# A hybrid decoder layer with a dense product-key expert stage: one-hot tiles stored token by token, lookups four places side by side, gate matrices in groups of 8 chunks

## The chip, the cores and the metric

The kernel runs on one core of one Trainium2 chip. A core has a matrix engine (TensorE, PE in the profile; PEld is its weight load), a vector engine (VectorE, DVE), a scalar engine (ScalarE, ACT), GpSimd (POOL) and a sync engine (SP) that only issues transfers. The metric is the device time of one execution in microseconds (us); lower is better. Before the change it was 1528.64 us, the median of 3 runs (1527.38 to 1529.46).

## What is computed (the reference)

One layer on 512 tokens of width 1024: a mixer (a short gated convolution and a gated linear recurrence side by side), then an expert stage whose "experts" are single neurons. The change lies in the expert stage alone:

```python
q = (xt @ wq).reshape(t, PEER_HEADS, 2, HALF_Q)                    # 8 heads, two halves each
scores = jnp.einsum('thpd,hpnd->thpn', q, keys)                    # 128 keys for each half
s_top, i_top = lax.top_k(scores, PEER_TOPK)                        # 16 best of each half
cand = s_top[:, :, 0, :, None] + s_top[:, :, 1, None, :]           # 16 x 16 pairs
c_score, c_idx = lax.top_k(cand, PEER_TOPK)                        # 16 best pairs
i1 = take_along_axis(i_top[:, :, 0], c_idx // 16); i2 = take_along_axis(i_top[:, :, 1], c_idx % 16)
expert = i1 * 128 + i2;  gates = softmax(c_score)
a = gelu(x . u_tab[expert]);  y = sum_k gates * a * v_tab[expert]  # 16384 experts, 8 x 16 per token
```

## The kernel before

There are four blocks of 128 tokens. Block 0 gathers the rows of its experts from u and v by indirect transfers (`gu`, `gv`, issued by GpSimd, computed on VectorE). Blocks 1 to 3 (TD = 384 tokens) are computed densely: all 16384 experts stand in 128 chunks of 128, and a matrix of gates G[token, expert], mostly zeros, weights them. Every fp32 product runs as three fp32r matmuls of split operands (`mm3`, L113; `split`, L96, makes the halves with one ScalarE and one VectorE instruction of 1024 columns).

- `uchunk(c)` (L439): loads 512 KB of u, splits it, 24 matmuls of 384 columns, a gelu on ScalarE. The result of the first 84 chunks (`SPILL`) goes to memory (`Ad`).
- `pick` and `lookup` (L543, L588): the top 16 pairs, then the two key numbers of each by a one-hot product: a [128, 16] tile `oh` (128 places, 16 candidates each) is compared, multiplied by the candidates' numbers `tif` and added up in halves.
- `gate_t(tb)` (L619) transposes key numbers and gates so that a partition is one of the 8 x 16 choices and a column a token, in fp16, with the gate in a high and a low part (tile `gt`).
- `gate_m(tb, b)` (L632), 24 calls: for 16 tokens it builds one-hot tiles in fp16 with four VectorE instructions (L643 to L646): `A` marks the first key, `B1` and `B2` the second key times the gate's high and low part. For each token two matmuls of 128x128 (L654, L655; `A` is the stationary operand, `B2` and `B1` are streamed) give its 128x128 gates; four tokens share a PSUM tile, which ScalarE copies to `stg` (L657). Every second call writes 2 MB to memory (`Gd`).
- The last stage (L757 on): chunks 84 to 127, then 0 to 83. `gload` brings gates of 4 chunks (768 KB) into a tile `Gt` (3 buffers); `vchunk` (L736) loads 512 KB of v, multiplies the gelu result by the gates (L742), splits it (L745, L747), and 18 matmuls of 512 columns add to six PSUM tiles. For the first 41 chunks of this stage a `uchunk` runs beside.

The program is written in a dependency framework: a scheduler reorders the instructions of each engine at build time, tiles take a pool's buffers and give them back after their last reader, and every engine then runs its list strictly in order. The list `work` (L702) interleaves u chunks with gate calls, `UOFF` (L43) says how many u chunks are kept back for after them, and 48 of the 256 gathers lie there too. In `gate_m` a token t of group q sits at `[:, q, :, t]` of a tile [128, 4, 128, 4], so one token's 128 values lie 4 elements (8 bytes) apart.

Of the kernel before, what the change touches and what calls it, by code (L numbers as in the profile page):

```python
# [21 lines left out]
P = 128  # L22
T = 512
# [16 lines left out]
TAIL = 4  # L40
EARLY = 48
PACE = (2.65, 1.1)
UOFF = 5  # L43
MRING = 12
STARTS = (16, 24, 29, 33, 36, 38, 40)
STEPS = (16, 8, 5, 4, 3, 2, 2)
# [7 lines left out]
def body(ctx, tc, a):  # L54
    nc = tc.nc
    V, S, G, PE = nc.vector, nc.scalar, nc.gpsimd, nc.tensor
# [8 lines left out]
    dr = sb("dr", space=DRAM)  # L65
# [53 lines left out]
    hT = (hp.tile([P, ND, T], F32R, tag="hi", name="hThi"), hp.tile([P, ND, T], F32R, tag="lo", name="hTlo"))  # L119
    x1d = dr.tile([NB, P, D], F32, name="x1d")  # L120
    h2d = dr.tile([P, D], F32, name="h2d")
    Gd = dr.tile([NK // 4, P, TD // CH, 4, CH], F32, name="Gd")
    Ad = dr.tile([SPILL, P, TD], F32, name="Ad")

    mp = sb("mp", 2)
# [262 lines left out]
    c = conv_c(0)  # L388
    for tb in range(NB):
        hgrn_pre(tb)  # L390
    for tb in range(NB):
# [8 lines left out]
        if tb < NB - 1:  # L400
            c = conv_c(tb + 1)
# [186 lines left out]
    def lookup(tb, j, picked):  # L588
        pa, pb, gs = picked
        idx = []  # L590
        for p_, pos in ((0, pa), (1, pb)):
            pos = pos[:, j * H * K:(j + 1) * H * K]
            ti = s2.tile([P, H, K], F16, tag="tif", name="tif")
            V.tensor_copy(ti, topi[tb][:, :, p_, :])
            oh = sp.tile([P, H * K, K], F16, tag="oh", name="oh")
            V.tensor_tensor(oh, pos.unsqueeze(2).to_broadcast([P, H * K, K]),
                            iota16[:, None, :].to_broadcast([P, H * K, K]), OP.is_equal)
            oh4 = oh.rearrange("p (h k) j -> p h k j", h=H)
            V.tensor_mul(oh4, oh4, ti.unsqueeze(2).to_broadcast([P, H, K, K]))
            V.tensor_add(oh[:, :, 0:8], oh[:, :, 0:8], oh[:, :, 8:16])  # L600
            V.tensor_add(oh[:, :, 0:4], oh[:, :, 0:4], oh[:, :, 4:8])
            V.tensor_add(oh[:, :, 0:2], oh[:, :, 0:2], oh[:, :, 2:4])
            ix = sp.tile([P, H * K], F32, tag="ix%d" % p_, name="ix")
            V.tensor_add(ix, oh[:, :, 0], oh[:, :, 1])
            idx.append(ix)
        return idx[0], idx[1], gs[j]

# [5 lines left out]
    gt = {}  # L613
# [5 lines left out]
    def gate_t(tb):  # L619
        i1, i2, g = lookup(tb, tb - 1, picked[0])  # L620
        o = ps()
        for j, t in enumerate((i1, i2, g)):
            PE.transpose(o[:, j * P:(j + 1) * P], t, ident)
        r = s2.tile([P, 4, P], F16, tag="gt", name="gt")
        S.activation(r[:, 0:2, :].rearrange("p a b -> p (a b)"), o[:, 0:2 * P], AF.Copy)
        S.activation(r[:, 2, :], o[:, 2 * P:3 * P], AF.Copy, scale=GSC)
        V.scalar_tensor_tensor(r[:, 3, :], o[:, 2 * P:3 * P], GSC, r[:, 2, :], op0=OP.mult, op1=OP.subtract)
        gt[tb] = r

    stg = {}  # L630

    def gate_m(tb, b):  # L632

        r = gt[tb]

        def view(j):
            return r[:, j, b * 16:(b + 1) * 16].rearrange("p (q t) -> p q t", t=4).unsqueeze(2).to_broadcast(
                [P, 4, NK, 4])
        io = iota4[:, None, :, :].to_broadcast([P, 4, NK, 4])
        A = s2.tile([P, 4, NK, 4], F16, tag="A", name="A")  # L640
        B1 = s2.tile([P, 4, NK, 4], F16, tag="B1", name="B1")
        B2 = s2.tile([P, 4, NK, 4], F16, tag="B2", name="B2")
# [218 lines left out]
```

## Time and profile before

| | |
|---|---|
| median of 3 runs | 1528.64 us |
| the profiled execution, its own time | 1528.5 us |
| its span, first to last instruction | 1526.7 us, mean granted clock 0.994 |
| busy: PE, PEld, DVE | 1502.8 (98%), 1338.8 (88%), 1213.2 (79%) us |
| busy: ACT, POOL | 638.8 (42%), 365.1 (24%) us |
| moved | 394.75 MB, mean 259 GB/s |

Busy time is the union of an engine's records. Each matmul's record is longer than its share of the engine, because matmuls overlap; what one costs in a stream is the distance from start to start. An idle stretch of an engine counts only where that engine ends last.

### The profile page before, as it was taken

The numbers are of one execution on the slowest core, as the hardware profiler recorded it, in microseconds if no ns is written. First come the engines' busy times: TensorE is split into PE (matmuls) and PEld (weight loads), VectorE is DVE, ScalarE is ACT, GpSimd is POOL, SyncE is SP. The second block draws the span as 40 slices with busy tenths as digits, with TensorE's granted clock in tenths as the row PEclk, the third lists the DMA queues.
The fourth block names the chain that finished last, engine by engine and source line by source line (L and its number), as shares of the span: only waits on it lengthen the run. The fifth ranks groups of instructions, "written<-read, shape, count | busy, mean of one in ns | idle before, by whom it ended". The sixth has DMA issues, their size and how long they took to land.

```text
span 1526.7 us, 21785 instructions
## 1 busy us (share of the span) xinstructions
PE 1502.8 (98%) x7929; PEld 1338.8 (88%) x7929; DVE 1213.2 (79%) x2312; ACT 638.8 (42%) x900; POOL 365.1 (24%) x300
## 2 busy tenths in 40 slices
PE   7999999999999999999999999999999999999997
PEld 6887777889999999999999999999998888888886
DVE  5847876899989988786646877888788888888888
ACT  5833324333543364655653333333333333333333
POOL 0000000000043311222004444444443332433330
PEclk9999999999999999999999999999999999999999
DMA  6221234523469788698759998988989999999993
GB/s 232 84 97 56 69 114 164 201 84 101 169 217 380 250 268 260 219 310 258 238 168 404 381 336 312 330 326 321 357 323 346 364 364 354 363 351 356 344 331 143
DMA packets 164652, 394.75 MB, mean 259 GB/s; under 512 B 13248, under 2 KB 84416, under 8 KB 164416
## 3 DMA queue, kind: packets, MB, share of 16 engines
q1 hardware_dynamic: 47520, 170.94, 30.8%
q0 software_dynamic: 41472, 159.40, 28.8%
q10 hardware_dynamic: 75552, 63.01, 13.0%
q8 instruction: 62, 1.02, 0.3%
q14 instruction: 46, 0.38, 0.1%
HBM read 346.90 MB, written 46.40 MB: 258 GB/s over the span
## 4 chain that ended last, share of the span: by engine, by line
PE 91%; DVE 5%; DMA 2%; ACT 1%; issue 1%; POOL 0%; DVEq 0%; ACTq 0%; SPq 0%; POOLq 0%
PE y L115 11%; PE y L116 11%; PE y L114 11%; PE pa L114 10%; PE pa L116 10%; PE pa L115 10%; PE pm L114 6%; PE pm L115 6%; PE pm L116 6%; PE pm L654 3%; PE pm L655 3%; DVE wlo L100 1%; PE pm L537 1%; DMA wraw<-in_u_dram,e_i 1%; PE pm L301 1%; DMA wraw<-in_v_l_dram 1%
## 5 line engine op out<-in xcount | busy, mean ns | idle before, releaser
L98 ACT ACTIVATE whi<-wraw 128x1024 fp32r<-128x1024 f32 x308 | 325.7, 1057 | 507.6 <-PE pa L115 199.0
L100 DVE TENSOR_TENSOR wlo<-wraw,whi 128x1024 fp32r<-128x1024 f32 x308 | 376.6, 1223 | 155.0 <-ACT whi L98 139.5
L114 PE MATMUL pa<-h2Thi,whi 128*128 128x384 f32 x1024 | 346.5, 338 | 4.1 <-ACT gl L446 4.1
L116 PE MATMUL pa<-h2Thi,wlo 128*128 128x384 f32 x1024 | 346.1, 338 | 0.0
L115 PE MATMUL pa<-h2Tlo,whi 128*128 128x384 f32 x1024 | 345.8, 338 | 0.0
L116 PE MATMUL y<-whi,wl 128*128 128x512 f32 x768 | 299.4, 390 | 0.0
L115 PE MATMUL y<-wlo,wh 128*128 128x512 f32 x768 | 299.3, 390 | 0.0
L114 PE MATMUL y<-whi,wh 128*128 128x512 f32 x768 | 297.9, 389 | 0.0
L673 POOL DMA_INDIRECT wraw<-in_u_dram,e_i x128 | 167.5, 1309 | 482.4 <-DMA Ad<-gl 178.4
L673 POOL DMA_INDIRECT wraw<-in_v_dram,e_i x128 | 175.4, 1370 | 303.5 <-DVE wlo L100 134.4
L114 PEld LDWEIGHTS pa<-h2Thi,whi 128*128 128x128 f32 x1024 | 193.9, 189 | 7.0 <-ACT gl L446 5.1
L115 PEld LDWEIGHTS pa<-h2Tlo,whi 128*128 128x128 f32 x1024 | 194.0, 189 | 1.6
L116 PEld LDWEIGHTS pa<-h2Thi,wlo 128*128 128x128 f32 x1024 | 193.8, 189 | 0.0
L687 DVE SCALAR_TENSOR_TENSOR y<-wraw,w,y 128x1024 f32<-128x1024 f32 x128 | 163.7, 1279 | 14.7 <-DMA wraw<-in_v_dram,e_i 14.6
L116 PEld LDWEIGHTS y<-whi,wl 128*128 128x128 f32 x768 | 144.2, 188 | 30.0
L745 ACT ACTIVATE wh<-w 128x384 fp32r<-128x384 f32 x128 | 67.0, 524 | 245.8 <-PE y L115 134.9
L114 PEld LDWEIGHTS y<-whi,wh 128*128 128x128 f32 x768 | 144.2, 188 | 29.1
L115 PEld LDWEIGHTS y<-wlo,wh 128*128 128x128 f32 x768 | 144.2, 188 | 29.0
L679 DVE SCALAR_TENSOR_TENSOR wraw<-wraw,h2n 128x1024 f32<-128x1024 f32 x128 | 155.8, 1219 | 15.2 <-DMA wraw<-in_u_dram,e_i 15.2
L747 DVE TENSOR_TENSOR wl<-w,wh 128x384 fp32r<-128x384 f32 x128 | 71.2, 557 | 41.7 <-ACT wh L745 38.2
L657 ACT ACTIVATE stg<-pm 128x512 f32<-128x512 f32 x96 | 94.2, 1162 | 21.5 <-PE pm L655 20.8
L654 PE MATMUL pm<-B,A 128*128 128x128 f16 x384 | 91.3, 297 | 0.0
(242 smaller groups left out, 1807.0 us busy)
## 6 DMA issues: line engine op xcount, KB each, us to landing
wraw<-in_u_l_dram SPq DMA_DIRECT2D x128, 512.0 KB
wraw<-in_v_l_dram SPq DMA_DIRECT2D x128, 512.0 KB
Gd<-stg ACTq DMA_DIRECT2D x12, 2048.0 KB
Gt<-Gd POOLq DMA_DIRECT2D x32, 768.0 KB
Ad<-gl ACTq DMA_DIRECT2D x84, 192.0 KB
glr<-Ad ACTq DMA_DIRECT2D x84, 192.0 KB
wraw<-in_w_in_dram SPq DMA_DIRECT2D x24, 512.0 KB
wraw<-in_wq_dram SPq DMA_DIRECT2D x16, 512.0 KB
```

The costliest lines, as they stand in the source:

```text
L98: S.activation(hi, src, AF.Copy)
L100: V.tensor_sub(lo, src, hi.bitcast(F32))
L114: PE.matmul(out, l[0], r[0], start=first, stop=False)
L115: PE.matmul(out, l[0], r[1], start=False, stop=False)
L116: PE.matmul(out, l[1], r[0], start=False, stop=last)
L654: PE.matmul(o3[:, t, :], A[:, q, :, t], B2[:, q, :, t], start=True, stop=False)
L657: S.activation(st[:, t0:t0 + 4, :], o3, AF.Copy, scale=1.0 / GSC)
L673: G.indirect_dma_start(out=t, out_offset=None, in_=a[tab], in_offset=bass.IndirectOffsetOnAxis(ap=e_i32[:, j:j + 1], axis=0))
L679: V.scalar_tensor_tensor(r, r, 1.0, h2n, op0=OP.mult, op1=OP.mult, accum_out=act0[:, j:j + 1])
L687: V.scalar_tensor_tensor(y0, r, w0[:, j:j + 1], y0, op0=OP.mult, op1=OP.add)
L745: S.activation(wh, w, AF.Copy)
L747: V.tensor_sub(wl, w, wh.bitcast(F32))
```

## The change

One-hot tiles are stored [128, 16 tokens, 64, 2]: the 128 values of a token lie side by side. The number that VectorE compares with is held twice in `gt` (the three instructions of `gate_t` that fill it write both copies), so that the innermost run is two equal fp16 values read again 64 times. In `lookup` the 16 candidates of four places lie side by side ([32, 16, 4]), and the sum ends one halving earlier. `Gd` and `Gt` hold 8 chunks in a group (`GC`), `Gt` has 2 buffers of 1536 KB in place of 3 of 768 KB, and `UOFF` goes from 5 to 8. `keys` moves into a buffer of `stg`.

```diff
-UOFF = 5
+GC = 8
+UOFF = 8
-    Gd = dr.tile([NK // 4, P, TD // CH, 4, CH], F32, name="Gd")
+    Gd = dr.tile([NK // GC, P, TD // CH, GC, CH], F32, name="Gd")
-    keys = sp.tile([P, NHP, NK], F32, name="keys")
+    keys = s2.tile([P, NHP, NK], F32, tag="stg", name="keys")
...
-            ti = s2.tile([P, H, K], F16, tag="tif", name="tif")
-            V.tensor_copy(ti, topi[tb][:, :, p_, :])
-            oh = sp.tile([P, H * K, K], F16, tag="oh", name="oh")
-            V.tensor_tensor(oh, pos.unsqueeze(2).to_broadcast([P, H * K, K]),
-                            iota16[:, None, :].to_broadcast([P, H * K, K]), OP.is_equal)
+            ti = s2.tile([P, H, K, 4], F16, tag="tif", name="tif")
+            V.tensor_copy(ti, topi[tb][:, :, p_, :].unsqueeze(3).to_broadcast([P, H, K, 4]))
+            oh = sp.tile([P, H * K // 4, K * 4], F16, tag="oh", name="oh")
+            V.tensor_tensor(oh.rearrange("p q (j r) -> p q j r", r=4),
+                            pos.rearrange("p (q r) -> p q r", r=4).unsqueeze(2).to_broadcast([P, H * K // 4, K, 4]),
+                            iota16.rearrange("p (j r) -> p j r", r=4).unsqueeze(1).to_broadcast(
+                                [P, H * K // 4, K, 4]), OP.is_equal)
...
-            V.tensor_add(oh[:, :, 0:8], oh[:, :, 0:8], oh[:, :, 8:16])
-            V.tensor_add(oh[:, :, 0:4], oh[:, :, 0:4], oh[:, :, 4:8])
-            V.tensor_add(oh[:, :, 0:2], oh[:, :, 0:2], oh[:, :, 2:4])
+            for n in (32, 16, 8):
+                V.tensor_add(oh[:, :, 0:n], oh[:, :, 0:n], oh[:, :, n:2 * n])
-            V.tensor_add(ix, oh[:, :, 0], oh[:, :, 1])
+            V.tensor_add(ix.rearrange("p (q r) -> p q r", r=4), oh[:, :, 0:4], oh[:, :, 4:8])
...
-        r = s2.tile([P, 4, P], F16, tag="gt", name="gt")
+        r = s2.tile([P, 4, P, 2], F16, tag="gt", name="gt")
+        o2 = o.unsqueeze(2).to_broadcast([P, T, 2])
...
-            return r[:, j, b * 16:(b + 1) * 16].rearrange("p (q t) -> p q t", t=4).unsqueeze(2).to_broadcast(
-                [P, 4, NK, 4])
+            return r[:, j, b * 16:(b + 1) * 16, :].unsqueeze(2).to_broadcast([P, 16, NK // 2, 2])
+        io = iota.rearrange("p (i r) -> p i r", r=2).unsqueeze(1).to_broadcast([P, 16, NK // 2, 2])
+        A, B1, B2 = (s2.tile([P, 16, NK // 2, 2], F16, tag=t, name=t) for t in ("A", "B1", "B2"))
...
-                PE.matmul(o3[:, t, :], A[:, q, :, t], B2[:, q, :, t], start=True, stop=False)
-                PE.matmul(o3[:, t, :], A[:, q, :, t], B1[:, q, :, t], start=False, stop=True)
+                one = [m[:, 4 * q + t].rearrange("p i r -> p (i r)") for m in (A, B2, B1)]
+                PE.matmul(o3[:, t, :], one[0], one[1], start=True, stop=False)
+                PE.matmul(o3[:, t, :], one[0], one[2], start=False, stop=True)
...
-        Gt[g] = vp.tile([P, TD // CH, 4, CH], F32, tag="G", name="Gt", bufs=3)
+        Gt[g] = vp.tile([P, TD // CH, GC, CH], F32, tag="G", name="Gt", bufs=2)
...
-    gload(order[0] // 4)
-    gload(order[0] // 4 + 1)
+    gs_ = []
+    for c in order:
+        if c // GC not in gs_:
+            gs_.append(c // GC)
+    gload(gs_[0])
+    used = []
     for n, c in enumerate(order):
-        if n % 4 == 0 and n // 4 + 2 < NK // 4:
-            gload(order[n + 8] // 4)
+        if c // GC not in used:
+            used.append(c // GC)
+            if len(used) < len(gs_):
+                gload(gs_[len(used)])
```

The built order on TensorE around the gate calls keeps its pattern: runs of 58 gate matmuls, and 6 a little ahead, for two calls. Elsewhere it moves at three places.

The first is GpSimd's list at the start of the last stage, where it loads the gates (`Gt`) ahead of the gathers of expert rows (`wraw`). Before:

```order
L734 DMA Gt_7904<-Gd_84 128x1536
L734 DMA Gt_7906<-Gd_84 128x1536
L734 DMA Gt_7908<-Gd_84 128x1536
L673 DMA wraw_7973<-in_u_dram,e_i32_2158 128x1024
L673 DMA wraw_7976<-in_v_dram,e_i32_2158 128x1024
```

And now:

```order
L736 DMA Gt_7904<-Gd_84 128x3072
L736 DMA Gt_7906<-Gd_84 128x3072
L675 DMA wraw_7971<-in_u_dram,e_i32_2158 128x1024
L675 DMA wraw_7974<-in_v_dram,e_i32_2158 128x1024
L675 DMA wraw_8040<-in_u_dram,e_i32_2158 128x1024
```

Three loads of 4 chunks become two of 8; 14 more follow, in place of 29.

The second is VectorE's list late in the last stage: `w` is the product with the gates (`glr` is the gelu result read back), `wl` and `wlo` are low halves of splits, `y0` is block 0's work. Before:

```order
L742 TENSOR_TENSOR w_13499<-glr_13491,Gt_13094 128x384
L747 TENSOR_TENSOR wl_13465<-w_13461,wh_13463 128x384
L100 TENSOR_TENSOR wlo_13459<-wraw_13455,whi_13457 128x1024
L679 SCALAR_TENSOR_TENSOR wraw_13523,act0_2160<-wraw_13523,h2n_2162 128x1024
L742 TENSOR_TENSOR w_13538<-glr_13530,Gt_13239 128x384
L747 TENSOR_TENSOR wl_13503<-w_13499,wh_13501 128x384
```

And now:

```order
L749 TENSOR_TENSOR wl_13473<-w_13469,wh_13471 128x384
L101 TENSOR_TENSOR wlo_13467<-wraw_13463,whi_13465 128x1024
L689 SCALAR_TENSOR_TENSOR y0_2163<-wraw_13600,w0_2161,y0_2163 128x1024
L689 SCALAR_TENSOR_TENSOR y0_2163<-wraw_13635,w0_2161,y0_2163 128x1024
L101 TENSOR_TENSOR wlo_13504<-wraw_13500,whi_13502 128x1024
L101 TENSOR_TENSOR wlo_13539<-wraw_13535,whi_13537 128x1024
L744 TENSOR_TENSOR w_13506<-glr_13498,Gt_13211 128x384
L744 TENSOR_TENSOR w_13541<-glr_13533,Gt_13211 128x384
L744 TENSOR_TENSOR w_13576<-glr_13568,Gt_13211 128x384
L744 TENSOR_TENSOR w_13611<-glr_13603,Gt_13211 128x384
L101 TENSOR_TENSOR wlo_13574<-wraw_13570,whi_13572 128x1024
```

Before, one product stood among each chunk's other work. Now four stand in a row, and the first of a group comes after the work on the group before it.

The third is the end of VectorE's list of these products. Now:

```order
L689 SCALAR_TENSOR_TENSOR y0_2163<-wraw_13846,w0_2161,y0_2163 128x1024
L689 SCALAR_TENSOR_TENSOR y0_2163<-wraw_13849,w0_2161,y0_2163 128x1024
L101 TENSOR_TENSOR wlo_13804<-wraw_13800,whi_13802 128x1024
L689 SCALAR_TENSOR_TENSOR y0_2163<-wraw_13852,w0_2161,y0_2163 128x1024
L744 TENSOR_TENSOR w_13786<-glr_13778,Gt_7904 128x384
L744 TENSOR_TENSOR w_13806<-glr_13798,Gt_7904 128x384
L744 TENSOR_TENSOR w_13823<-glr_13815,Gt_7904 128x384
L744 TENSOR_TENSOR w_13840<-glr_13832,Gt_7904 128x384
```

The last four chunks (80 to 83) belong to the group that was loaded first (`Gt_7904`, chunks 80 to 87). That tile keeps one of the two buffers through the whole stage, so the 14 groups after the second pass one after another through the other buffer: GpSimd's load of a group waits for VectorE's eighth product of the one before (`Gt_8190` and those after it have such a wait; the first two have none of it).

## Rows read from the trace of the kernel before

**Rows 1.** The page, busy time by engine (share of the span, instructions).

```profile
PE 1502.8 (98%) x7929; PEld 1338.8 (88%) x7929; DVE 1213.2 (79%) x2312; ACT 638.8 (42%) x900; POOL 365.1 (24%) x300
```

**Rows 2.** Windows: length, busy us of PE, PEld, DVE, ACT, POOL, clock, DMA share.

```profile
370.00:430.00 60.00, 60.00 (x348) 60.00 (x347) 60.00 (x345) 27.41 (x35) 0.00 (x0) 1.00 0.49 164
515.00:600.00 85.00, 85.00 (x550) 82.57 (x549) 73.49 (x77) 44.65 (x54) 20.51 (x11) 1.00 0.77 251
515.00:787.00 272.00, 272.00 (x1808) 263.58 (x1807) 206.06 (x202) 155.28 (x187) 50.75 (x23) 1.00 0.77 245
820.00:1162.00 342.00, 342.00 (x1735) 311.79 (x1734) 279.54 (x350) 126.22 (x172) 151.12 (x123) 1.00 0.92 339
1162.00:1503.00 341.00, 341.00 (x1506) 282.47 (x1505) 287.91 (x380) 124.43 (x171) 116.80 (x107) 1.00 0.95 349
```

**Rows 3.** Chain that ended last, 515 to 790 us, shares by line.

```profile
by line: PE pa L114 22.3%; PE pa L116 22.3%; PE pa L115 22.2%; PE pm L654 16.6%; PE pm L655 16.5%; PE pm L623 0.2%
```

**Rows 4.** Timeline of PE in a gate run: start, length (us).

```profile
661.01 0.30 PE L654 MATMUL pm<-B,A 128*128 128x128 f16 x1
...
661.96 0.30 PE L655 MATMUL pm<-B,A 128*128 128x128 f16 x1
```

**Rows 5.** Timeline of PE, 384 columns; 25 steps from first to last.

```profile
650.06 0.33 PE L114 MATMUL pa<-h2Thi,whi 128*128 128x384 f32 x1
...
654.39 0.33 PE L115 MATMUL pa<-h2Tlo,whi 128*128 128x384 f32 x1
```

**Rows 6.** Timeline of PE, 512 columns; 8 steps from first to last.

```profile
1300.03 0.39 PE L116 MATMUL y<-whi,wl 128*128 128x512 f32 x1
...
1301.84 0.39 PE L115 MATMUL y<-wlo,wh 128*128 128x512 f32 x1
```

**Rows 7.** Weight loads of single lines, ns: least/median/most.

```profile
L655 PEld LDWEIGHTS <-A x384: 112/117/135, 535.8 to 785.8; 128*128 128x128 f16 x192
L285 PEld LDWEIGHTS pm<-Q,E x32: 190/192/192, 105.9 to 110.7; 128*128 128x128 f32 x32
L320 PEld LDWEIGHTS po<-F,Q x64: 106/108/109, 119.6 to 202.8; 128*32 128x32 f32 x64
```

**Rows 8.** Timeline of PE, eight fp32 matmuls merged: start, length.

```profile
106.01 1.06 PE L285 MATMUL pm<-Q,E 128*128 128x128 f32 x8
```

**Rows 9.** Groups by line: count, busy us, mean ns, idle before.

```profile
L657 ACT ACTIVATE stg<-pm 128x512 f32<-128x512 f32 x96 | 94.2, 1162 | 21.5 <-PE pm L655 20.8 <-ACT gl L446 0.4 <-issue 0.3
L643 DVE TENSOR_TENSOR A<-iota,gt 128x2048 f16<-128x2048 f16 x24 | 29.3, 1223 | 20.1 <-PE pm L655 18.3 <-ACT gt L625 1.8
L596 DVE TENSOR_TENSOR oh<-pb,iota 128x2048 f16<-128x2048 f16 x4 | 9.2, 2294 | 0.1
L602 DVE TENSOR_TENSOR oh<-oh 128x256 f16<-128x256 f16 x8 | 3.6, 446 | 0.0
L601 DVE TENSOR_TENSOR oh<-oh 128x512 f16<-128x512 f16 x8 | 3.5, 442 | 0.0
L604 DVE TENSOR_TENSOR ix<-oh 128x128 f32<-128x128 f16 x8 | 3.4, 429 | 5.9 <-PE pm L623 5.9
```

**Rows 10.** Windows behind a wait of PE: columns as in Rows 2.

```profile
450.00:455.00 5.00, 1.91 (x12) 1.59 (x10) 5.00 (x13) 3.03 (x4) 4.09 (x4) 0.92 0.65 206
455.00:460.00 5.00, 5.00 (x16) 5.00 (x17) 5.00 (x14) 1.44 (x2) 3.80 (x4) 0.50 0.88 275
```

**Rows 11.** The gate products of the last 84 chunks: first and last start.

```profile
L742 DVE TENSOR_TENSOR w<-glr,Gt x84: 546/553/561, 1162.2 to 1502.7; 128x384 f32<-128x384 f32 x84
```

**Rows 12.** Chain of waits, 425 to 470 us: a 512 KB gather landing.

```profile
430.40 4.50 DMA wraw<-in_u_dram,e_i
```

**Rows 13.** Chain of waits, 787 to 830 us: a 512 KB load landing.

```profile
807.84 9.30 DMA wraw<-in_v_l_dram
```

More of the change, by code (lines that the diff above doesn't have):

```diff
@@ L505, in ps @@
         return psS.tile([P, T], F32, tag="m", name="pm")
-    keys = sp.tile([P, NHP, NK], F32, name="keys")
+    keys = s2.tile([P, NHP, NK], F32, tag="stg", name="keys")
     S.dma_start(out=keys, in_=a["keys"])
-    iota4 = sp.tile([P, NK, 4], F16, name="iota4")
-    S.dma_start(out=iota4, in_=a["iota4"])
-    iota16 = sp.tile([P, K + 240], F16, name="iota16")[:, 0:K]
+    iota = sp.tile([P, NK + 128], F16, name="iota")[:, 0:NK]
+    S.dma_start(out=iota, in_=a["iota"])
+    iota16 = sp.tile([P, 4 * K + 192], F16, name="iota16")[:, 0:4 * K]
     S.dma_start(out=iota16, in_=a["iota16"])
@@ L592, in lookup @@
             pos = pos[:, j * H * K:(j + 1) * H * K]
-            ti = s2.tile([P, H, K], F16, tag="tif", name="tif")
-            V.tensor_copy(ti, topi[tb][:, :, p_, :])
-            oh = sp.tile([P, H * K, K], F16, tag="oh", name="oh")
-            V.tensor_tensor(oh, pos.unsqueeze(2).to_broadcast([P, H * K, K]),
-                            iota16[:, None, :].to_broadcast([P, H * K, K]), OP.is_equal)
-            oh4 = oh.rearrange("p (h k) j -> p h k j", h=H)
-            V.tensor_mul(oh4, oh4, ti.unsqueeze(2).to_broadcast([P, H, K, K]))
-            V.tensor_add(oh[:, :, 0:8], oh[:, :, 0:8], oh[:, :, 8:16])
-            V.tensor_add(oh[:, :, 0:4], oh[:, :, 0:4], oh[:, :, 4:8])
-            V.tensor_add(oh[:, :, 0:2], oh[:, :, 0:2], oh[:, :, 2:4])
+            ti = s2.tile([P, H, K, 4], F16, tag="tif", name="tif")
[5 more added lines that the diff above has]
+                                [P, H * K // 4, K, 4]), OP.is_equal)
+            oh4 = oh.rearrange("p (h q) x -> p h q x", h=H)
+            V.tensor_mul(oh4, oh4, ti.rearrange("p h j r -> p h (j r)").unsqueeze(2).to_broadcast(
+                [P, H, K // 4, K * 4]))
+            for n in (32, 16, 8):
+                V.tensor_add(oh[:, :, 0:n], oh[:, :, 0:n], oh[:, :, n:2 * n])
             ix = sp.tile([P, H * K], F32, tag="ix%d" % p_, name="ix")
-            V.tensor_add(ix, oh[:, :, 0], oh[:, :, 1])
+            V.tensor_add(ix.rearrange("p (q r) -> p q r", r=4), oh[:, :, 0:4], oh[:, :, 4:8])
             idx.append(ix)
@@ L623, in gate_t @@
             PE.transpose(o[:, j * P:(j + 1) * P], t, ident)
-        r = s2.tile([P, 4, P], F16, tag="gt", name="gt")
-        S.activation(r[:, 0:2, :].rearrange("p a b -> p (a b)"), o[:, 0:2 * P], AF.Copy)
-        S.activation(r[:, 2, :], o[:, 2 * P:3 * P], AF.Copy, scale=GSC)
-        V.scalar_tensor_tensor(r[:, 3, :], o[:, 2 * P:3 * P], GSC, r[:, 2, :], op0=OP.mult, op1=OP.subtract)
+        r = s2.tile([P, 4, P, 2], F16, tag="gt", name="gt")
+        o2 = o.unsqueeze(2).to_broadcast([P, T, 2])
+        S.activation(r[:, 0:2].rearrange("p a b r -> p (a b) r"), o2[:, 0:2 * P], AF.Copy)
+        S.activation(r[:, 2], o2[:, 2 * P:3 * P], AF.Copy, scale=GSC)
+        V.scalar_tensor_tensor(r[:, 3], o2[:, 2 * P:3 * P], GSC, r[:, 2], op0=OP.mult, op1=OP.subtract)
         gt[tb] = r
@@ L636, in view @@
         def view(j):
-            return r[:, j, b * 16:(b + 1) * 16].rearrange("p (q t) -> p q t", t=4).unsqueeze(2).to_broadcast(
-                [P, 4, NK, 4])
[L639 to L642, printed above, removed]
+            return r[:, j, b * 16:(b + 1) * 16, :].unsqueeze(2).to_broadcast([P, 16, NK // 2, 2])
+        io = iota.rearrange("p (i r) -> p i r", r=2).unsqueeze(1).to_broadcast([P, 16, NK // 2, 2])
+        A, B1, B2 = (s2.tile([P, 16, NK // 2, 2], F16, tag=t, name=t) for t in ("A", "B1", "B2"))
         V.tensor_tensor(A, io, view(0), OP.is_equal)
@@ L647, in gate_m @@
         if b % 2 == 0:
-            stg[0] = s2.tile([P, NK // 4, 4, CH], F32, tag="stg", name="stg")
+            stg[0] = s2.tile([P, NK // GC, GC, CH], F32, tag="stg", name="stg")
         st = stg[0].rearrange("p g c t -> p t (g c)")
@@ L742, in vchunk @@
         V.tensor_mul(w.rearrange("p (b t) -> p b t", t=CH), gl.rearrange("p (b t) -> p b t", t=CH),
-                     Gt[c // 4][:, :, c % 4, :])
+                     Gt[c // GC][:, :, c % GC, :])
         wh = vp.tile([P, TD], F32R, tag="wh", name="wh", bufs=4)
@@ L849 @@
         scanm=c(np.broadcast_to((np.arange(T) % CH != 0).astype(np.float32), (P, T))),
-        iota4=c(np.broadcast_to(pos[None, :, None], (P, P, 4)).astype(np.float16)),
-        iota16=c(np.broadcast_to(np.arange(K)[None, :], (P, K)).astype(np.float16)),
+        iota=c(np.broadcast_to(pos[None, :], (P, P)).astype(np.float16)),
+        iota16=c(np.broadcast_to(np.repeat(np.arange(K), 4)[None, :], (P, 4 * K)).astype(np.float16)),
     )
```

## The prediction

> **What bounds the kernel now.** I read the page first: TensorE is busy for 98% of the span, VectorE for 79%, ScalarE for 42% [rows 1]. An engine at 98% over the whole span leaves one question to the windows: is it so in the stage that is changed? It is. Between 515 and 787 us, where all gate calls lie, TensorE is busy for 272 of 272 us, VectorE for 206 and ScalarE for 155; in the last stage (820 to 1503 us) TensorE is again never idle, VectorE is at 82 to 84% and the DMA engines at 92 to 95% [rows 2]. The chain of waits confirms that busy means bound: from 515 to 790 us it runs through TensorE alone, and 33.1% of it, 91.0 us, are the two gate matmul lines L654 and L655 [rows 3]. So a microsecond taken from those lines is a microsecond of the kernel, until VectorE, ScalarE or a transfer becomes late instead; and a microsecond of VectorE in this stage is worth nothing yet.
>
> **The change part by part.**
>
> *Gate matmuls (768, L654 and L655).* 91.0 us over 768 is 118.5 ns each. The timeline agrees: eight steps from 661.01 to 661.96 us are 119 ns each [rows 4]. What would they cost with the 128 values side by side? No fp16 matmul with adjacent values is in the trace, so I take the nearest streams, the fp32r ones, whose values are adjacent: 384 columns take 4.33 us over 25 steps, 173.2 ns [rows 5]; 512 columns take 1.81 over 8, 226.3 ns [rows 6]. That is 0.415 ns for a column and 14 ns beside; for 128 columns the line gives 67 ns. A gate matmul costs 51 ns more than this, about another 128 x 0.415: it streams at half the rate. Its weight load could forbid 67 ns: its record is 117 ns [rows 7], suspiciously near the 118.5. But a record of a load holds latency that overlaps: the fp32 load of 128 columns has 192 ns, yet eight such matmuls follow each other in 1.06 us, some 112 ns apart [rows 7, 8]. Of fp32 loads 32 columns take 108 ns and 128 take 192, so some 80 ns are fixed [rows 7]; that leaves 37 of the 117 ns for occupying the array, under 67. I take 67 ns: 768 x 51.5 = 39.6 us saved. The bounds are 118.5 (nothing saved) and 0.415 x 128 = 53 ns (50 us).
>
> [...]
>
> *Gate tiles on VectorE (96 instructions, L643 to L646).* Same element counts, 2048 each. Now the broadcast number is read as a run of four fp16 values again and again, at 1.22 us [rows 9]; then it is a run of two. An instruction whose broadcast operand has no such run (L596, one value read 16 times) takes 2.29 us for the same 2048 [rows 9]. These are the bounds: no change, or 96 x 1.07 = 103 us more. I take no change, since two adjacent values still fill the pair that the faster rate handles; it is the nearer row.
>
> *Lookups (8 one-hot products).* L596 gets a run of four and should fall from 2.29 to the 1.22 us of L643: 8.6 us of VectorE. The last two additions lose their short runs (446 and 429 ns [rows 9]); at best they become a third cheaper, 2 us together. The cast that fills `tif` grows from 128 to 512 elements: at most the 0.44 us of L601 for 512, 3.5 us in all [rows 9]. Net some 5 to 10 us of VectorE, worth nothing on the path: even where VectorE has no free time (370 to 430 us) TensorE stays full [rows 2].
>
> *gate_t and the copies to `stg`.* Six instructions write twice as many values; the 96 copies of 1162 ns [rows 9] keep their pattern. Nothing.
>
> *What is late next in the gate stage.* 272 - 40 = 232 us of TensorE stand against VectorE's 206 less 3 lookup pairs, some 200 us, and ScalarE's 155. On average TensorE still ends last. It is tight at the start: from 515 to 600 us VectorE has 73 of 85 us [rows 2], and TensorE would give up 10 to 13. I add 3 us for waits there (0 to 10). Against it works that VectorE itself waited 18.3 us for TensorE to free `A` [rows 9]; that shrinks. UOFF moves three u chunks from the stage to behind it, but the built order has only one chunk more between the last gate matmul and the first v matmul: nothing.
>
> *Gate loads in groups of 8.* Bytes stay, loads become 16 of 1536 KB. But `Gt_7904` holds a buffer to the end, so from the third group on a load starts only when VectorE's eighth product is done. How much cover has it? In the last 84 chunks a chunk takes (1502.7 - 1162.2)/83 = 4.10 us [rows 11]. The products come in fours; behind the eighth, VectorE still owes splits and low halves for four chunks and TensorE has these four to run, 16 us, plus the rest of the four before. I count 20 us from the load's issue until TensorE runs dry. The landing: 512 KB take 4.5 us in a quiet stretch [rows 12] and 9.3 in the most crowded one [rows 13]; three times that is 13.5 to 28 us. I take 14 to 18: covered, with 2 us in all for stragglers. In the first 41 chunks each takes twice as long, so the cover doubles there.
>
> *Sum.* The profiled execution took 1528.5 us (span 1526.7 and 1.8 around it), 0.1 below the median of the runs, so I sum against it: 1528.5 - 39.6 + 3 + 2 = 1494 us.
>
> **The rivals.**
>
> *One buffer for the gates is too few.* Ten loads fall in the last 84 chunks. If a load lands at the upper bound, 28 us, each leaves 8 us of TensorE idle: 80 us, 1574. For it: the DMA engines are 95% busy there [rows 2] and gathers queue on the same GpSimd list. Against: the same traffic feeds TensorE without any gap now, and while VectorE waits, the other loads fill their buffers and stop. [...] I price this case at 2.5 us a load: 1494 + 25 - 2 = 1517. It turns slower from 3.6 us a load on.
>
> *VectorE loses its fast rate on runs of two (the slower case).* Then 200 + 103 = 303 us of VectorE stand in the gate stage and TensorE no longer bounds it: 303 in place of 272, 1528.5 + 31 = 1560. For it: L602, whose runs are pairs, takes 446 ns for 256 elements, while L601 takes 442 for 512 [rows 9], so pairs went at half rate there. Against: L604, single values 32 bytes apart, needs 429 ns for 128 [rows 9], so distance alone slows a read, and the gate tiles have none: the pair is read again in place, the rest is contiguous. Slower begins where VectorE passes 272 us, at (272 - 200)/96 = 0.75 us more per instruction.
>
> *The stride is not why the stream is slow.* If each gate matmul waits for its own 117 ns load, or fp16 streams so in any layout, nothing is saved: 1528.5 + 0 to 3, no change. For it: 117 beside 118.5. Against: the fp32 loads above. [...]
>
> **How the numbers follow.** The sum holds: 69%, 1483 (53 ns a matmul) to 1503 (waits of 10 us in the gate stage and 4 in the last one). One buffer too few: 13%, 1503 to 1574, mostly under 1520 (10 faster, 1 same, 2 slower). Slow pairs: 9%, slower. No gain: 9% (7 same; 2 faster, where only a part of the rate comes back). The range for 8 in 10 is 1482 to 1520; outside lie slow pairs, no gain and the worst of the single buffer. About 0.2% (3 us) can be told from no change. Faster: 69 + 10 + 2 = 81%. Same: 1 + 7 = 8%. Slower: 9 + 2 = 11%.
>
> **What would show it.** Right: L654 and L655 start some 67 ns apart and their records fall from 0.30 us [rows 4] to about 0.23; L643 to L646 stay at 1.22 us and L596 falls to it; TensorE's gate stage takes 230 to 240 us, and it stays at 100% after 820 us. Wrong: gate matmuls still 118 ns apart (no gain); L643 to L646 near 2.3 us with TensorE waiting for `B` (slow pairs); in the last stage, VectorE waiting for a `Gt` transfer every eighth chunk and TensorE idle behind it (one buffer).

## The result and the profile after

The changed kernel takes 1499.96 us (median of 6 runs, 1497.07 to 1507.19), the one before 1528.61 (6 runs on the same chip). The medians lie 28.6 us apart. The ratio, which is taken of the means, is 0.9826, with a 95% interval from 0.9801 to 0.9851: 1.7% faster. The forecast was 1494, its range 1482 to 1520. The profiled execution took 1500.03 us, its span 1498.1.

Line numbers have moved: the gate matmuls are L656 and L657 now, the gate tiles L644 to L647, the copies to `stg` L659, the gelu L447, its store to `Ad` L449, `mm3` L115 to L117, the products of the last stage L744.

First the gate matmuls. The timeline of PE in a gate run (start, length in us) answers to [rows 4]:

```profile
705.34 0.22 PE L656 MATMUL pm<-B,A 128*128 128x128 f16 x1
705.40 0.22 PE L657 MATMUL pm<-B,A 128*128 128x128 f16 x1
705.46 0.22 PE L656 MATMUL pm<-B,A 128*128 128x128 f16 x1
```

They start some 56 ns apart (the median over the run; the times here are rounded to 10 ns) where they started 119 apart. The groups by line, 300 to 850 us (count, busy us, mean ns of one, idle time before), answer to [rows 7, 9]:

```profile
L657 PEld LDWEIGHTS <-A 128*128 128x128 f16 x384 | 34.9, 98 | 2.0 <-issue 1.9
L644 DVE TENSOR_TENSOR A<-iota,gt 128x2048 f16<-128x2048 f16 x24 | 29.3, 1221 | 6.3 <-ACT gt L629 4.3 <-PE pm L657 2.0
L597 DVE TENSOR_TENSOR oh<-pb,iota 128x2048 f16<-128x2048 f16 x4 | 4.9, 1216 | 0.0
L659 ACT ACTIVATE stg<-pm 128x512 f32<-128x512 f32 x96 | 92.3, 1156 | 17.7 <-PE pm L657 17.7
```

VectorE's gate tiles with runs of two cost 1.22 us, what runs of four did [rows 9], the lookups' compare fell from 2.29 to 1.22 us, and the copies to `stg` are as before (1156 ns, 1162 [rows 9]).

The windows (length, busy us of PE, PEld, DVE, ACT, POOL, clock, DMA share) answer to [rows 2]:

```profile
515.00:600.00 85.00, 82.01 (x626) 78.79 (x625) 74.44 (x79) 48.13 (x59) 27.79 (x10) 1.00 0.84 283
515.00:760.00 245.00, 234.36 (x1826) 224.67 (x1825) 198.35 (x198) 154.90 (x188) 53.37 (x22) 0.99 0.79 272
794.00:1136.00 342.00, 342.00 (x1730) 311.22 (x1729) 277.20 (x345) 123.40 (x169) 149.57 (x119) 1.00 0.91 334
1136.00:1478.00 342.00, 341.79 (x1509) 282.65 (x1508) 287.71 (x382) 124.97 (x174) 115.17 (x96) 1.00 0.93 347
```

TensorE was full in the matching windows before [rows 2]. Now it is full, to 0.2 us, in the last stage alone, and lacks 10.6 us between 515 and 760. The waits of PE from 515 to 850 us (total us, times, longest) say for what:

```profile
PE pa L115 <- ACT gl L447: 8.2, 7, 3.2
PE pm L656 <- DVE B L646: 1.8, 1, 1.8
PE pm L657 <- DVE B L647: 0.3, 1, 0.3
```

`gl` is the gelu that empties the PSUM buffer of a u chunk; the kernel before has one such wait in this stretch and no other:

```profile
PE pa L114 <- ACT gl L446: 1.0, 1, 1.0
```

The chain of waits ran through TensorE alone before [rows 3]. Now, from 525 to 752 us, ScalarE's copies are its largest line, with 24.6%, and TensorE's matmuls together hold 57%:

```profile
by line: ACT stg L659 24.6%; PE pa L115 17.0%; PE pa L116 16.1%; PE pa L117 16.0%; issue 4.9%; DMA Gd<-stg 4.8%; PE pm L656 4.3%; PE pm L657 3.4%; ACTq L449 2.7%; ACT gl L447 2.2%; ACT whi L99 1.1%; ACTq L662 0.7%; DVE A L644 0.5%; DVE wlo 
```

Why a gelu of 0.48 us is late shows in the timeline of ScalarE around the longest wait (ACTq is its queue issuing a DMA):

```profile
619.82 7.68 ACT L659 ACTIVATE stg<-pm 128x512 f32<-128x512 f32 x8 [1.77 <-PE pm L657]
627.53 0.38 ACTq L662 DMA_DIRECT2D Gd<-stg  x1
628.01 0.49 ACT L447 ACTIVATE gl<-pa 128x384 f32<-128x384 f32 x1 [0.51 <-ACT stg L659]
628.53 6.08 ACTq L449 DMA_DIRECT2D Ad<-gl  x1
634.71 1.06 ACT L99 ACTIVATE whi<-wraw 128x1024 fp32r<-128x1024 f32 x1 [5.26 <-issue]
635.67 0.47 ACT L447 ACTIVATE gl<-pa 128x384 f32<-128x384 f32 x1
636.18 0.35 ACTq L449 DMA_DIRECT2D Ad<-gl  x1
```

Two things can hold it. Copies stand in rows of up to eight ahead of it, and behind the store of the gates (L662) the issue of the next small store (L449) takes 6.08 us instead of the 0.35 of the one after it, with everything on ScalarE behind it. TensorE then starts at 636.20 after 3.19 us without work, and pays again:

```profile
635.00:640.00 5.00, 3.80 (x12) 3.70 (x12) 5.00 (x6) 2.58 (x4) 0.00 (x0) 0.54 1.06 393
```

The granted clock of these 5 us is 0.54; behind the wait of [rows 10] it was 0.50. The blocked issue is no child of the change. Before, it is there behind every one of the 12 stores, 2.9 to 5.2 us each, 51 us together. One of them, in the timeline of ScalarE of the kernel before:

```profile
544.66 0.38 ACTq L660 DMA_DIRECT2D Gd<-stg  x1
...
546.61 5.10 ACTq L448 DMA_DIRECT2D Ad<-gl  x1
```

It cost nothing there: from 545 to 553 us TensorE ran matmuls of u chunks without a gap. That it is the slow gate matmuls which left ScalarE this time is shown by e7 below. After the change an issue in this stage exceeds 0.8 us 8 times, 18 us together. Each store writes rows of 1 KB in place of 512 bytes; on the queue that carries them, q10, packets fell from 75552 to 50976:

```profile
q10 hardware_dynamic: 50976, 62.93, 11.9%
```

**Where the time went.** I add up TensorE's steps (start of a matmul to start of the next) from 300 us on, in three heaps: steps from a gate matmul, steps over 0.4 us (waits, and what the start behind them costs), and all others. The same for every run below. It is one profiled execution of each, up to 6 us from the median of its runs:

```
profiled run                          gate   long  other    span (us)
before                                87.3    5.2  1125.6  1526.7
after                                 42.4   21.1  1124.8  1498.1
e1  token tiles alone                 42.1   42.1  1127.6  1522.3
e2  after, groups of 4                42.4   32.5  1124.6  1507.8
e3  after, store on SyncE             43.0   20.6  1124.2  1497.6
e4  after, copies in runs of 4        42.7   21.6  1124.6  1498.6
e5  after, UOFF 5                     45.3   36.7  1123.6  1515.4
e6  after, old lookups                42.6   26.0  1122.9  1501.5
e7  after, moving operand strided     85.6    5.7  1124.4  1525.6
e8  after, stationary one strided     43.3   25.1  1124.0  1502.4
e9  after, old one-hot tiles          87.5    7.0  1121.1  1525.4
e10 e3 and e4 together                42.8   11.5  1124.6  1488.7
e11 e10, fewer early gathers          43.5   28.9  1125.3  1507.9
e12 e1, with the edits of e10         42.7   19.8  1126.8  1499.8
```

From before to after the gate matmuls give 44.9 us, and 15.9 come back as long steps: 29.0 net, against 28.6 in the span.

### The profile page after: what moved, and what is told of

It is laid out like the page before. It is cut to its first block, busy times and chain, and to the rows that moved or that the text cites. A ratio compares the mean times of both kernels' runs of the same rounds, so it can differ in the third digit from the quotient of the medians.

```text
span 1498.1 us, 21741 instructions
## 1 busy us (share of the span) xinstructions
PE 1462.3 (98%) x7929; PEld 1297.3 (87%) x7929; DVE 1201.3 (80%) x2312; ACT 637.0 (43%) x900; POOL 365.8 (24%) x284
## 3 DMA queue, kind: packets, MB, share of 16 engines
q10 hardware_dynamic: 50976, 62.93, 11.9%
## 4 chain that ended last, share of the span: by engine, by line
PE 76%; DVE 6%; ACT 5%; issue 5%; DMA 5%; POOL 2%; ACTq 1%; POOLq 0%; DVEq 0%
PE y L116 10%; PE y L115 10%; PE y L117 10%; PE pa L115 8%; PE pa L116 7%; PE pa L117 7%; PE pm L115 7%; PE pm L116 6%; PE pm L117 6%; ACT stg L659 4%; DMA wraw<-in_v_dram,e_i 2%; POOL wraw L675 2%; DVE wlo L101 2%; DMA wraw<-in_u_dram,e_i 1%; PE pm L538 1%
## 5 line engine op out<-in xcount | busy, mean ns | idle before, releaser
L115 PE MATMUL pa<-h2Thi,whi 128*128 128x384 f32 x1024 | 348.0, 340 | 12.7 <-ACT gl L447 12.4
L117 PE MATMUL pa<-h2Thi,wlo 128*128 128x384 f32 x1024 | 346.6, 338 | 0.0
L675 POOL DMA_INDIRECT wraw<-in_u_dram,e_i x128 | 183.3, 1432 | 490.2 <-DVE ci L523 178.6
L115 PE MATMUL y<-whi,wh 128*128 128x512 f32 x768 | 298.9, 389 | 0.2 <-ACT wh L747 0.2
L117 PE MATMUL y<-whi,wl 128*128 128x512 f32 x768 | 296.8, 390 | 0.0
L675 POOL DMA_INDIRECT wraw<-in_v_dram,e_i x128 | 169.4, 1323 | 263.2 <-DVE wlo L101 122.0
L115 PEld LDWEIGHTS pa<-h2Thi,whi 128*128 128x128 f32 x1024 | 194.3, 190 | 17.8 <-ACT gl L447 15.9
L117 PEld LDWEIGHTS pa<-h2Thi,wlo 128*128 128x128 f32 x1024 | 194.1, 190 | 0.0
L117 PEld LDWEIGHTS y<-whi,wl 128*128 128x128 f32 x768 | 144.1, 188 | 30.2
L115 PEld LDWEIGHTS y<-whi,wh 128*128 128x128 f32 x768 | 144.2, 188 | 29.7 <-ACT wh L747 0.6
L659 ACT ACTIVATE stg<-pm 128x512 f32<-128x512 f32 x96 | 92.3, 1156 | 17.7 <-PE pm L657 17.7
L115 PE MATMUL pm<-hThi,whi 128*128 128x512 f32 x192 | 77.7, 406 | 8.4 <-ACT whi L99 8.4
```

The costliest lines, as they stand in the source:

```text
L115: PE.matmul(out, l[0], r[0], start=first, stop=False)
L117: PE.matmul(out, l[1], r[0], start=False, stop=last)
L675: G.indirect_dma_start(out=t, out_offset=None, in_=a[tab], in_offset=bass.IndirectOffsetOnAxis(ap=e_i32[:, j:j + 1], axis=0))
```

## The experiments

Theory: reading the moving operand in place brings 45 us; waits of TensorE in the gate stage, mostly for what ScalarE's queue holds up, take a share of it back, and the other three edits decide how large that share is. Rivals: the token tiles are all that matters; the single spare gate buffer took the rest; VectorE did. Each run has a ratio to the kernel before on its own chip, and where it is set against the changed kernel, that is done by these ratios. The lists of the engines are built anew for every variant. By line and tile TensorE's list is the changed kernel's in e4, e7 and e8, and in e2 up to 1140 us; in the others it differs in the gate stage.

**e1, the token tiles alone** (kernel before with the new `gate_t` and `gate_m`; lookups, groups of 4 and UOFF 5 stay):

```diff
-                PE.matmul(o3[:, t, :], A[:, q, :, t], B2[:, q, :, t], start=True, stop=False)
+                one = [m[:, 4 * q + t].rearrange("p i r -> p (i r)") for m in (A, B2, B1)]
+                PE.matmul(o3[:, t, :], one[0], one[1], start=True, stop=False)
```

> Kernel before with the token-by-token one-hot tiles alone (old lookups, groups of 4 chunks, UOFF 5). Theory: the tiles bring the gate matmuls to the full rate (records 0.22 us, about 40 us less of TensorE), but the store of the gate matrices keeps its 512-byte rows, behind which ScalarE's issue of the spilled gelu was held up 3 to 5 us after each of the 12 stores in the kernel before (only up to 6 us in 5 places after). TensorE, no longer slowed by the stride, now waits for the gelu behind them: 1503 to 1512 us, 18 to 25 less than before, longer than the changed kernel. Rival A, only the tiles matter and the groups of 8 are worth nothing: 1498 to 1502. Rival B, the layout is not the source of the gain: about 1528.

Measured: 1526.53 us, ratio 0.9996 (0.9980 to 1.0013): no change, as rival B had it. But the table denies B's reason. The gate matmuls are at full rate (42.1 us), and 36.9 us stand against them in long steps. Waits of PE, 515 to 850 us, then the longest on ScalarE's side and the clock behind it:

```profile
PE pa L114 <- ACT gl L446: 21.0, 17, 7.5
PE pm L653 <- ACT stg L656: 4.3, 3, 2.4
```

```profile
640.25 10.37 ACTq L448 DMA_DIRECT2D Ad<-gl  x1
```

```profile
645.00:650.00 5.00, 0.00 (x0) 0.00 (x0) 4.46 (x4) 0.00 (x0) 0.00 (x0) 0.87 1.12 373
650.00:655.00 5.00, 2.79 (x9) 2.79 (x10) 3.19 (x3) 2.87 (x4) 1.68 (x1) 0.50 0.89 329
```

All 12 issues behind a store are blocked again, 3.7 to 10.4 us each, 56 us in all. The theory had the place right and the size too small. (3.8 us of the waits lie at the very end, 1474 to 1499 us; they are in e12 too.)

**e2, groups of 4 again** (`GC = 4`, three `Gt` buffers, loads two groups ahead).

> Changed kernel with the gate matrices in groups of 4 chunks again (three buffers, loads two groups ahead). Theory: twice as many store rows, ScalarE's issues behind the stores are held up 3 to 5 us at all 12, TensorE's waits in the gate stage grow from about 10 to 15 or 20 us: 1504 to 1512. Rival A: regrouping is worth nothing either way, 1498 to 1502. Rival C, the single spare Gt buffer costs time in the changed kernel: then this kernel is faster, under 1497.

Measured: 1509.89 us, ratio 0.9896 (0.9875 to 0.9917), some 11 us slower than the changed kernel. So rival C falls: with three buffers it is not faster. TensorE's list in the gate stage is the same here, so no new order on TensorE explains the loss. The waits for the gelu are 19.1 us in place of 8.2, and again 12 issues are blocked, 51 us together:

```profile
PE pa L115 <- ACT gl L447: 19.1, 16, 5.4
PE pm L656 <- ACT stg L659: 2.4, 2, 2.1
```

**e5, UOFF 5, and e6, the old lookups,** each put back alone in the changed kernel.

> Changed kernel with UOFF 5 in place of 8 (three more u chunks lie among the gate calls). The token tiles alone measured 1526.5 us and the changed kernel with groups of 4 1509.9; between these two lie only UOFF and the lookups, 16 us. Theory now: both kernels lose the same 40 us of gate matmuls and differ in TensorE's waits for the gelu and the slow clock behind them. Theory U, UOFF is what tells: each u chunk moved out of the stage takes its gelu, its split and its issue off ScalarE and VectorE there, so with 5 the waits grow from 10.6 to some 18 to 20 us: 1506 to 1512. Theory L, the lookups tell: no change from the changed kernel, 1498 to 1502.

> Changed kernel with the old lookups (single values, 2.29 us for the compare). Theory U (UOFF explains the 16 us): VectorE does 8 to 10 us more, TensorE's waits grow by 0 to 3 us: 1499 to 1503. Theory L (the lookups, whose 10 us lie just ahead of a third of the gate calls each, are what VectorE lacks): 1508 to 1514.

Measured: e5 1511.50 us, ratio 0.9890 (0.9861 to 0.9920), about 10 us slower than the changed kernel; e6 1505.36, ratio 0.9877 (0.9852 to 0.9903), about 8 us slower, with an interval that begins 0.0001 above the end of the changed kernel's. Neither theory U nor L alone holds: putting back either costs time. But TensorE's list differs from the changed kernel's at some 20 places in either, so each price is that of the edit together with its new order. In e5 it is mostly VectorE that is late: 15.6 us of TensorE's 20.9 us of waits are for it, 5.3 for ScalarE (waits of PE, 515 to 850 us; then VectorE's own, 515 to 760 us):

```profile
PE pm L656 <- DVE B L646: 11.7, 8, 6.1
```

```profile
DVE wraw L681 <- DMA wraw<-in_u_dram,e_i: 24.8, 7, 7.8
DVE y L689 <- DMA wraw<-in_v_dram,e_i: 13.1, 5, 5.1
```

The longest of these, 7.79 us, stands between two gate tiles (670.94 and 684.11 us), and TensorE waits 6.13 us behind it. In e6 the profiled gate stage waits hardly longer (9.1 us for the gelu); 5.0 us of waits lie at 1370 and 1405 us, where the changed kernel has none. TensorE's list differs there too, from 1147 us on; how lookups near 500 us lead to that, no run says. The two profiled executions lie only 3.4 us apart.

**e9, the three other edits without the token tiles.**

```diff
-                one = [m[:, 4 * q + t].rearrange("p i r -> p (i r)") for m in (A, B2, B1)]
+                PE.matmul(o3[:, t, :], A[:, q, :, t], B2[:, q, :, t], start=True, stop=False)
```

> Changed kernel with the old one-hot tiles (four tokens interleaved): lookups, groups of 8 and UOFF 8 without the token layout. Token tiles alone measured no change; taking out any one of the other three from the changed kernel cost 7 to 12 us. Theory, the three only shorten waits that a faster TensorE would run into: with 118 ns a gate matmul TensorE has no such waits, so they are worth 0 to 3 us here: 1524 to 1529. Rival, they are worth their 7 to 12 us each in any company: 1500 to 1508.

Measured: 1531.62 us, ratio 1.0034 (1.0018 to 1.0050), even 5 us slower, a little above the theory's range; I have no cause for those 5, the profiled run does not have them (span 1525.4). With 118 ns a gate matmul TensorE is full in the gate stage, so there is nothing that the three could shorten:

```profile
515.00:850.00 335.00, 335.00 (x2150) 324.48 (x2149) 237.45 (x244) 180.45 (x221) 72.26 (x44) 1.00 0.76 275
```

So the tiles alone bring nothing, the other three bring nothing, and together they bring 28.6 us.

**e7 and e8, which operand.** In both the operand takes every fourth value of four tokens' tiles, in e7 the moving one (B, the two tiles numbered 1 and 2 below), in e8 the stationary one (A, number 0); the diff is that of e7:

```diff
+                wide_ = [m[:, 4 * q + t // 4 * 4:4 * q + t // 4 * 4 + 4].rearrange("p t i r -> p (t i r)") for m in (A, B2, B1)]
+                one = [wide_[n][:, t % 4::4] if n in (1, 2) else one[n] for n in range(3)]
```

> Changed kernel, where only the moving operand of the gate matmuls (B) is read 8 bytes apart: every fourth value of four tokens' tiles in place of one token's 128 values (so the gate values differ; the counts and shapes are the same). Theory M, the moving stream sets the pace: the gate matmuls are 118 ns apart again, their records 0.30 us, the profiled span about 1524 to 1528. Rival S, the weight load of a strided stationary operand set it: 54 to 70 ns apart and a span of 1496 to 1501.

> Changed kernel, where only the stationary operand of the gate matmuls (A) is read 8 bytes apart (every fourth value of four tokens' tiles; the gate values differ, the counts are the same). Theory M (the moving stream sets the pace): as the changed kernel, 54 to 70 ns apart, a span of 1496 to 1501, and the weight load's record 117 ns again if the stride is what lengthens it. Rival S: 118 ns apart, 1524 to 1528.

Measured (one timed run each): e7 1527.82 us, gate matmuls 115 to 116 ns apart; e8 1504.75 us, 56 ns apart. Theory M holds. Groups by line of e7, then of e8:

```profile
L658 PE MATMUL pm<-B,A 128*128 128x128 f16 x384 | 89.2, 293 | 0.0
L659 PEld LDWEIGHTS <-A 128*128 128x128 f16 x384 | 44.1, 115 | 2.1 <-issue 1.9
```

```profile
L659 PE MATMUL pm<-B,A 128*128 128x128 f16 x384 | 42.2, 220 | 0.6 <-DVE B L647 0.6
L659 PEld LDWEIGHTS <-A 128*128 128x128 f16 x384 | 39.5, 114 | 2.0 <-issue 1.9
```

The load's record of 114 ns means nothing for the pace: with it the matmuls still run 56 ns apart in e8, whose time lies among those of the changed kernel (1497.07 to 1507.19).

e7 also shows what hid ScalarE before. TensorE's list is that of the changed kernel, and the edit changes only how B is read; five issues on ScalarE are still blocked in the stage, 11.5 us together, and TensorE waits for nothing:

```profile
515.00:850.00 335.00, 335.00 (x2166) 326.27 (x2165) 240.94 (x248) 178.26 (x221) 70.45 (x43) 1.00 0.76 272
```

**e3, the store issued by SyncE, and e4, copies in runs of four,** the two direct cures for ScalarE's queue:

```diff
-            S.dma_start(out=Gd[:, :, blk].rearrange("g p c t -> p g (c t)"),
+            nc.sync.dma_start(out=Gd[:, :, blk].rearrange("g p c t -> p g (c t)"),
```

```diff
-            S.activation(st[:, t0:t0 + 4, :], o3, AF.Copy, scale=1.0 / GSC)
+            S.activation(st[:, t0:t0 + 4, :].rearrange("p t i -> p i t"), o3.rearrange("p t i -> p i t"),
+                         AF.Copy, scale=1.0 / GSC)
```

> Changed kernel with the store of the gate matrices issued by SyncE in place of ScalarE. Theory: the issue of the spilled gelu is no longer held up behind the store (each under 0.6 us in place of up to 6.1), the TensorE wait of 3.2 us at 633 us and parts of the others go; the eight evictions in a row ahead of a gelu stay: 1493 to 1498. Rival D, the order of evictions and gelu on ScalarE is the whole of the waits: 1499 to 1501. Rival E, the store now holds up the weight loads on SyncE by as much: 1502 to 1508.

> Changed kernel, where the eviction of four tokens' gate matrices runs over the columns outside and the four tokens inside, so that it writes runs of four values and reads PSUM 512 bytes apart (same result). Theory: if the 128-byte step of the writes is what makes it 1156 ns, it falls to 0.6 to 0.8 us, the blocks of eight evictions ahead of a gelu from 9 to about 6 us, and TensorE's waits in the gate stage from 10 to about 5: 1493 to 1497. Rival F, the eviction is bound elsewhere (1.1 us or more): 1499 to 1502; if the strided reading of PSUM is worse, above 1.3 us and over 1502.

Measured: e3 1502.02 us, ratio 0.9841 (0.9819 to 0.9864), no gain; e4 1496.69, ratio 0.9804 (0.9783 to 0.9826), not to be told from the changed kernel (0.9801 to 0.9851). Both do what they should to ScalarE: in e3 no issue there is over 0.8 us, in e4 a copy takes 621 ns in place of 1156 (group by line, 515 to 790 us):

```profile
L659 ACT ACTIVATE stg<-pm 128x512 f32<-128x512 f32 x96 | 48.7, 621 | 21.5 <-PE pm L657 19.5 <-issue 1.9
```

But the wait changes hands. In e3 the gelu still holds TensorE for some of its time, and VectorE for more than before (PE, 515 to 850 us):

```profile
PE pa L115 <- ACT gl L447: 6.0, 6, 1.6
PE pm L656 <- DVE B L646: 5.4, 2, 2.7
```

In e4 the gelu no longer appears, though nine issues are still blocked there, 24 us together: shorter copies alone were enough to bring it in time. VectorE appears in its place (PE, 515 to 850 us; then VectorE before a gate tile, 6.72 us for a gathered row):

```profile
PE pm L656 <- DVE B L646: 7.6, 3, 5.2
PE pm L657 <- DVE B L647: 1.4, 3, 0.9
```

```profile
650.96 1.28 DVE L690 SCALAR_TENSOR_TENSOR y<-wraw,w,y 128x1024 f32<-128x1024 f32 x1 [6.72 <-DMA wraw<-in_v_dram,e_i]
652.16 1.22 DVE L644 TENSOR_TENSOR A<-iota,gt 128x2048 f16<-128x2048 f16 x1
```

**e10, both cures; e12, both cures on the token tiles alone.**

> Changed kernel with evictions in runs of four values (0.62 us in place of 1.16) and the store of the gate matrices issued by SyncE. Theory: ScalarE's two hold-ups of the gelu go both; what is left are TensorE's waits for B on VectorE (5 to 9 us, behind rows gathered late): 1490 to 1496. Rival, the waits only move: as either one alone, 1496 to 1502.

> Kernel before with the token tiles alone, as the first experiment, and in it the two edits that relieve ScalarE's queue directly: evictions in runs of four values and the store of the gate matrices issued by SyncE (old lookups, groups of 4, UOFF 5). Theory: the 45 us of gate matmuls were lost to waits of TensorE for the gelu behind evictions and blocked issues on ScalarE; with these gone most of the gain returns without the three other edits: 1494 to 1506, where the tiles alone had 1526.5. Rival, VectorE or the end of the kernel took it (old lookups, three more u chunks in the stage, waits for B): 1515 to 1527.

Measured: e10 1494.36 us, ratio 0.9781 (0.9764 to 0.9798), faster than both kernels: its interval ends below that of the changed one. e12 1501.50, ratio 0.9828 (0.9799 to 0.9857), where the tiles alone had 0.9996. The two kernels e1 and e12 differ by these two edits (and TensorE's list, built anew, at 15 places between 587 and 683 us), and 25 us come back: in e1 it was ScalarE's queue that took the gain. Waits of PE, 515 to 850 us, in e10 and then in e12:

```profile
PE pm L656 <- DVE B L646: 4.8, 1, 4.8
```

```profile
PE pm L653 <- DVE B L643: 8.1, 4, 5.2
PE pa L114 <- ACT gl L446: 0.6, 1, 0.6
```

The hold-up has not gone, it moved with the store. In e12 SyncE's issue of a load of u right behind a store takes up to 5.41 us (at 642.36 us), in e10 up to 3.80, in e3 up to 1.98. Among TensorE's waits in the stage none of these loads appears.

**e11, fewer gathered rows in the gate stage** (on e10):

```diff
-EARLY = 48
+EARLY = 32
     for c in range(nu, SPILL):
         uchunk(c)
+        take(2)
```

> As the run before it (evictions in runs of four, store on SyncE), and of the 48 gathered rows of the gate stage 16 move behind the last gate call, two to each u chunk there (EARLY 32). Theory: VectorE no longer waits some 5 us at a time for a gathered row ahead of the gate tiles, TensorE's waits for B halve: 1486 to 1492. Rival: rows that VectorE waited for are as late elsewhere, and the order is made anew with as many waits: 1492 to 1500.

Measured: 1514.26 us, ratio 0.9922 (0.9896 to 0.9947), 20 us slower than e10; the theory fell. TensorE's waits for B stayed (5.2 us against 5.0), and waits for the low half of a split (7.1 us) and for the gelu (5.0) came on top. VectorE waited 50 us for gathered rows in the stage, 20 times, where e10 waited 15.4 us, 5 times (VectorE's waits, 515 to 770 us, e11):

```profile
DVE wraw L682 <- DMA wraw<-in_u_dram,e_i: 30.7, 10, 5.4
DVE y L690 <- DMA wraw<-in_v_dram,e_i: 19.3, 10, 6.6
```

The trace reads as if not the number of gathers told but how soon behind its issue the order uses one: the gather issued at 578.58 us is wanted at 579.65 and used at 586.23, and gate tiles stand behind that product. GpSimd could not issue it sooner: it had waited 5.96 us for VectorE to be done with an earlier row (`wraw`, L682). No run tests this by itself.

## Why the prediction came out as it did

*Gate matmuls: mechanism right, term too small.* The sum had 67 ns each and 39.6 us saved; measured are 56 ns, and 44.9 us over the steps (less than 768 times the difference, because the step from the last gate matmul of a run to the next line was short already, 51 ns before and 31 after). The part that was off is the 14 ns "beside" a column's 0.415 ns: it came from a line through two fp32r widths [rows 5, 6], and for fp16 columns in sequence 56 less 128 x 0.415 leaves 3 ns. The lower bound, 53 ns, was nearly the value. The weight load did not forbid it, as argued, and e8 shows it with the long load record (114 ns) in place.

*The stride is the reason.* e7 settles the third rival: moving operand back to 8-byte steps, pace back to 115 ns, against 56 in sequence. For the stationary operand nothing was lost at the same step (56 ns in e8).

*Waits in the gate stage: the term that was mis-sized most.* The sum had 3 us, 10 at most, and put them at the start of the stage, on VectorE. Measured are 15.9 us of longer steps, spread over the stage and mostly on ScalarE: an engine at 155 us of 272 [rows 2] that I compared by its busy time. Its queue is in order, its copies come in rows of up to eight (7.68 us of them ahead of the gelu at 628.01 us), and the 51 us of blocked issues are not in the busy time at all, since issuing counts as none. The 5.10 us row was there to be read before.

*"Worth nothing on the path": wrong for all three other edits, together.* Lookups, UOFF and groups of 8 were each priced against the kernel before, where they are worth nothing (e9). Against the changed kernel, and each with the order that it brings, they are worth some 8, 10 and 11 us (e6, e5, e2), and without them the tiles would have gained nothing (e1). The regrouping was costed only by its loads in the last stage; its effect is in the gate stage, where e2 shows it with the same list on TensorE and 12 blocked issues again. That the sum still missed by only 6 us is luck in part: 5 us more were saved than forecast, 13 us of waits were overlooked, and 2 us for gate loads were not needed.

*Gate tiles on VectorE: right,* 1.22 us with runs of two, as with runs of four, where single values took 2.29 [rows 9], so the slow-pairs rival falls.

*One gate buffer: no cost, as forecast, though the landing was sized too long.* 14 to 18 us were taken; the median of 16 is 9.7 (DMA issues: KB each, us to landing), and VectorE waited 2.8 us for it in all (group of its products):

```profile
Gt<-Gd POOLq DMA_DIRECT2D x16, 1536.0 KB, 9.7
```

```profile
L744 DVE TENSOR_TENSOR w<-glr,Gt 128x384 f32<-128x384 f32 x84 | 43.0, 552 | 8.4 <-issue 5.3 <-DMA Gt<-Gd 2.8
```

TensorE's longest wait from 794 to 1478 us is 0.2 us. No run shows the 2.5 us a load at which the rival was priced: it was the author's estimate, and in its place stand these 2.8 us of VectorE for all 16 loads.

## What to carry to other kernels

When the engine that bounds a stage gets faster, price every other edit against the kernel that results, not against the one that is: what is hidden now may be the next bound. Before believing that an engine has slack, look past its busy time at its queue, at the issue rows and at how long a small urgent instruction stands behind a row of long ones. And read a moving operand in sequence (here 56 ns a matmul, against 115 with 8-byte steps); if a tile must be interleaved for one reader, interleave the stationary one (56 ns in e8).

## What the runs showed of the hardware

- A DMA issue can hold up the engine that issues it for long: on ScalarE 0.33 us is the median, 2.9 to 10.4 us were taken right behind a store of 512-byte rows (before, e1), up to 6.1 behind one of 1 KB rows (after). With the store on SyncE no issue of ScalarE in the gate stage was over 0.5 us (e3, e10, e12), and SyncE's next issue took up to 5.4 (e12). What inside the queue blocks it, no row says.
- A ScalarE copy from PSUM of 128x512 took 1156 ns with writes 128 bytes apart (after), and 621 ns with runs of four values and PSUM read 512 bytes apart (e4). The reads took on the long step and the copy still fell, so the step of the writes was the price.
- A fp16 matmul of 128 columns with a weight load before each ran every 56 ns (after), also with the stationary operand 8 bytes apart (e8), and every 115 to 116 ns with the moving one so (e7).
